# An instance norm on one core: the last pair of rows of each tile normalised by VectorE and ScalarE together

## The chip, the core and the metric

The kernel runs on one core of a Trainium2 chip. The time is device microseconds (us) for one execution of the whole kernel. Six runs of the kernel before took 5006.07, 5009.72, 4999.88, 4965.09, 4964.45 and 4966.33 us; the median is 4983.1 us. The profile is of one further execution, which took 4963.64 us.

Names used: DVE is VectorE, ACT is ScalarE, SP is SyncE (here it only issues transfers), DMA stands for the core's 16 DMA engines. HBM is the memory outside the core, SBUF the large memory inside it, PSUM the small one.

## The reference

```python
x: float32 [256, 256, 4096]          # np.random.randn
eps: 1e-5

mean = np.mean(x, axis=2, keepdims=True)
var = np.var(x, axis=2, keepdims=True)
return ((x - mean) / np.sqrt(var + eps)).astype(np.float32)
```

There are 65,536 independent rows of 4096 float32. Each row is read once from HBM and written once: 1073.74 MB in, 1073.74 MB out.

## The kernel before

**Tiles.** A tile holds 512 rows: 128 partitions with K = 4 rows each, 64 KB per partition, 8.39 MB in all. There are 128 tiles and three buffers (`X[0]` to `X[2]`) in SBUF. Tile t lives in buffer t mod 3, and the normalised rows overwrite the loaded ones.

**VectorE, per tile** (`vector_tile`). It waits for the load, then runs one pass per row (L86, four of them) that multiplies the row by 1/4096 in place and accumulates its sum, so that the row's mean comes out beside it. Then, for each pair of rows, it waits until ScalarE has the pair's standard deviation, takes the reciprocal (L97), works out minus mean times reciprocal (L99), and normalises the two rows in place with one multiply-add pass each (L108).

**ScalarE, per tile** (`scalar_tile`). As each row's mean arrives it squares the row's deviation from it and accumulates the sum (L132, output thrown away into `junk` in PSUM). After each second row it takes a square root over two columns (L141), which releases VectorE for that pair.

**SyncE** issues every transfer, all on one queue, in an order written out by hand. In the steady part it repeats: wait until tile t is done and store it (L155), then wait until the store of tile t-1 has landed, since that frees the buffer, and load tile t+2 into it (L160). The wait for "tile t is done" counts the four increments that the four L108 instructions give to `done`.

**Ends.** The first tile is loaded in two halves of two rows each, and the first and the last tile are computed and stored in halves (L171), so that the first store can begin early and the last store is short. At the start SyncE issues the two half loads, the load of tile 1, the two half stores of tile 0, the load of tile 2, and then goes on as above. At the end the last load is issued two tiles ahead, and the stores of the last three tiles follow.

Engines speak to one another only through semaphores: `loaded`, `means`, `stds`, `done`, `stored`. A semaphore called `scaled` is allocated and not used. `take` waits for a count and then clears the semaphore.

Of the kernel before, what the change touches and what calls it, by code (L numbers as in the profile page):

```python
# [10 lines left out]
def kernel(  # L11
# [9 lines left out]
    AF = mybir.ActivationFunctionType  # L21
    ALU = mybir.AluOpType
    P = 128
    K = 4
    BUFS = 3

    x_flat = x.flatten_outer_dims()
    out_flat = out.flatten_outer_dims()
    n, d = x_flat.shape
# [7 lines left out]
    half = K // 2  # L37
# [7 lines left out]
    junk = psum.tile([P, d], fp32)  # L45
    X = [pool.tile([P, K, d], fp32, name=f"x{s}") for s in range(BUFS)]
    mean, ss, std, rstd, nbias = (
        [pool.tile([P, K], fp32, name=f"{name}{s}") for s in range(BUFS)]
        for name in ("mean", "ss", "std", "rstd", "nbias")
    )  # L50
# [3 lines left out]

    loaded = [nc.alloc_semaphore(f"loaded{s}") for s in range(BUFS + 1)]
    stored = [nc.alloc_semaphore(f"stored{s}") for s in range(BUFS + 1)]
    own_v = nc.alloc_semaphore("own_v")
# [3 lines left out]
    scaled = nc.alloc_semaphore("scaled")  # L61
    done = [nc.alloc_semaphore(f"done{s}") for s in range(BUFS + 1)]
    ready = nc.alloc_semaphore("ready")

    def take(engine, sem, count):
        engine.wait_ge(sem, count)
        engine.sem_clear(sem)  # L67

    V, A, S = nc.vector, nc.scalar, nc.sync

    def vector_tile(s, r0=0, k=K, ld=None, dn=None):

        x = X[s]
        ld = loaded[s] if ld is None else ld
        dn = done[s] if dn is None else dn
        own = 0

        def mine(instruction):
            nonlocal own
            own += 1  # L80
            return instruction.then_inc(own_v, 1)

        if ld:
            take(V, ld, 16)
        for r in range(r0, r0 + k):
            V.tensor_scalar(  # L86
                out=x[:, r, :], in0=x[:, r, :], scalar1=1.0 / d, scalar2=None, op0=ALU.mult, op1=ALU.add,
                accum_out=mean[s][:, r : r + 1],
            ).then_inc(means, 1)
        for b in range(r0, r0 + k, 2):  # L90
            c = slice(b, b + 2)
            final = b == r0 + k - 2
            if final:
                take(V, stds, (b - r0) // 2 + 1)
            else:
                V.wait_ge(stds, (b - r0) // 2 + 1)
            mine(V.reciprocal(out=rstd[s][:, c], in_=std[s][:, c]))  # L97
            V.wait_ge(own_v, own)
            mine(V.scalar_tensor_tensor(  # L99
                out=nbias[s][:, c], in0=mean[s][:, c], scalar=-1.0 / d, in1=rstd[s][:, c], op0=ALU.mult, op1=ALU.mult  # L100
            ))
            if final:
                take(V, own_v, own)
            else:
                V.wait_ge(own_v, own)
            for r in range(b, b + 2):
                c = slice(r, r + 1)
                V.tensor_scalar(  # L108
                    out=x[:, r, :], in0=x[:, r, :], scalar1=rstd[s][:, c], scalar2=nbias[s][:, c],
                    op0=ALU.mult, op1=ALU.add,  # L110
                ).then_inc(dn, 1)

    def scalar_tile(s, r0=0, k=K, ld=None, dn=None):

        x = X[s]
        last = r0 + k - 1
        own = 0

        def mine(instruction):
            nonlocal own  # L120
            own += 1
            return instruction.then_inc(own_a, 1)

        for r in range(r0, last + 1):
            c = slice(r, r + 1)
            if own:
                A.wait_ge(own_a, own)
            if r == last:
                take(A, means, k)
            else:  # L130
                A.wait_ge(means, r - r0 + 1)
            mine(A.activation(  # L132
                out=junk, in_=x[:, r, :], func=AF.Square, bias=mean[s][:, c], scale=-float(d), accum_out=ss[s][:, c]
            ))
            if (r - r0) % 2:
                c = slice(r - 1, r + 1)
                if r == last:
                    take(A, own_a, own)
                else:
                    A.wait_ge(own_a, own)  # L140
                A.activation(  # L141
                    out=std[s][:, c], in_=ss[s][:, c], func=AF.Sqrt, bias=eps_tile, scale=1.0 / d**3
                ).then_inc(stds, 1)

    def rows_of(ap, t):

        if isinstance(t, int):
            return ap[t]
        first, period, count, i = t
        ap = ap[first : first + period * (count - 1) + 1 : period]  # L150
        return ap[bass.ds(i, 1)].rearrange("o p k d -> p (o k) d")

    def store(s, t):
        take(S, done[s], K)
        S.dma_start(out=rows_of(out_t, t), in_=X[s][:, :, :]).then_inc(stored[s], 16)  # L155

    def load(s, t, wait=True):
# [4 lines left out]
    def half_of(h):  # L162
        return slice(h * half, (h + 1) * half)

    def second(sems, s, h):
        return sems[BUFS] if h else sems[s]

    def store_half(s, t, h):
        r = half_of(h)
        take(S, second(done, s, h), half)  # L170
        S.dma_start(out=out_t[t][:, r, :], in_=X[s][:, r, :]).then_inc(second(stored, s, h), 16)  # L171

    def halves(tile_fn, s, first):
# [4 lines left out]
    last = ntiles - 1  # L178
# [3 lines left out]
    with tc.tile_critical():  # L182
        with nc.Block() as block:  # L183

            @block.sync
            def _(sync):
                for h in range(2):
                    r = half_of(h)
                    S.dma_start(out=X[0][:, r, :], in_=x_t[0][:, r, :]).then_inc(second(loaded, 0, h), 16)
                load(1, 1, wait=False)  # L190
                store_half(0, 0, 0)
                store_half(0, 0, 1)
                load(2, 2, wait=False)
                store(1, 1)
                take(S, stored[BUFS], 16)
                load(0, 3)

                with S.Fori(0, rounds) as i:
                    for t in range(L0, L0 + BUFS):
                        store(t % BUFS, (t, BUFS, rounds, i))  # L200
                        load((t + 2) % BUFS, (t + 2, BUFS, rounds, i))
                load(last % BUFS, last)
                store((last - 2) % BUFS, last - 2)
                store((last - 1) % BUFS, last - 1)
                store_half(last % BUFS, last, 0)
                store_half(last % BUFS, last, 1)
                for s in ((last - 2) % BUFS, (last - 1) % BUFS, last % BUFS, BUFS):
                    take(S, stored[s], 16)

            @block.vector  # L210
            def _(vector):
                V.memset(eps_tile, eps / d**2).then_inc(ready, 1)  # L212
                halves(vector_tile, 0, True)
                vector_tile(1)
                with V.Fori(0, rounds) as i:
                    for j in range(BUFS):
                        vector_tile((L0 + j) % BUFS)
                vector_tile((last - 2) % BUFS)
                vector_tile((last - 1) % BUFS)
                halves(vector_tile, last % BUFS, False)  # L220

            @block.scalar
            def _(scalar):
                take(A, ready, 1)
                halves(scalar_tile, 0, True)
                scalar_tile(1)
                with A.Fori(0, rounds) as i:
                    for j in range(BUFS):
                        scalar_tile((L0 + j) % BUFS)
                scalar_tile((last - 2) % BUFS)  # L230
                scalar_tile((last - 1) % BUFS)
                halves(scalar_tile, last % BUFS, False)
# [35 lines left out]
```

## Time and profile before

| what | value |
|---|---|
| median of six runs | 4983.1 us (4964.45 to 5009.72) |
| profiled execution, own time | 4963.64 us |
| its span, first to last instruction | 4961.6 us |
| DVE busy | 3506.0 us (71% of the span), 2049 instructions |
| ACT busy | 2024.4 us (41%), 1282 instructions |
| moved by DMA | 2147.52 MB, mean 433 GB/s |
| one L108 pass over 128x4096 (DVE) | 2410 ns |
| one L132 pass over 128x4096 (ACT) | 3678 ns |
| one L86 pass over 128x4096 (DVE) | 4416 ns |

A busy share is a share of the span in which the engine executed something. The digits of the slice rows are tenths: 9 stands for 90% or more of one fortieth of the span. "Issue to landing" of a transfer is the time from the moment SyncE issues it until its last byte is reported; it contains the time that the transfer spends behind others.

### The profile page before, as it was taken

How to read it: one execution, taken by the hardware profiler on the slowest of the kernel's cores; microseconds unless marked ns; L12 is line 12 of the kernel's file. 1: busy time of each engine (PE TensorE's matmuls, PEld its weight loads, DVE VectorE, ACT ScalarE, POOL GpSimd, SP SyncE). 2: the span in 40 equal slices, each digit the busy share in tenths (PEclk: the TensorE clock that was granted, in tenths of full speed). 3: DMA queues.
4: the chain of work that ended last, by engine and by line, in shares of the span. 5: the costliest groups of instructions: out<-in, count | busy, mean ns of one | idle time of the engine just before them, and what ended most of it. 6: DMA issues, size and time to landing. Idle time of an engine off the chain costs nothing.

```text
span 4961.6 us, 5694 instructions
## 1 busy us (share of the span) xinstructions
DVE 3506.0 (71%) x2049; ACT 2024.4 (41%) x1282; POOL 0.2 (0%) x4
## 2 busy tenths in 40 slices
DVE  6777767777677766777667776777767776677766
ACT  4444333443344433444334443344334443344433
POOL 0000000000000000000000000000000000000000
DMA  9999999999999999999999999999999999999999
GB/s 414 435 434 431 436 431 432 435 434 435 433 434 436 432 434 436 433 433 435 434 436 433 434 436 432 434 435 434 434 435 434 435 433 434 435 433 434 435 434 405
DMA packets 37298, 2147.52 MB, mean 433 GB/s; under 512 B 4144, under 2 KB 4144, under 8 KB 4144
## 3 DMA queue, kind: packets, MB, share of 16 engines
q1 hardware_dynamic: 37296, 2147.50, 100.0%
q14 instruction: 2, 0.02, 0.0%
HBM read 1073.74 MB, written 1073.74 MB: 433 GB/s over the span
## 4 chain that ended last, share of the span: by engine, by line
DMA 73%; DVE 25%; issue 1%; another core or an unknown queue 0%; ACT 0%; SPq 0%; DVEq 0%; ACTq 0%
DMA x<-in_x_dram 41%; DMA out_dram<-x 32%; DVE x L86 16%; DVE x L108 8%; DVE nbias L99 0%; ACT junk L132 0%; DVE rstd L97 0%; DVEq L67 0%; SPq L160 0%; SPq L155 0%; DVEq L183 0%; ACT std L141 0%; SPq L67 0%; ACT L141 0%
## 5 line engine op out<-in xcount | busy, mean ns | idle before, releaser
L86 DVE TENSOR_SCALAR_CACHE_REDUCE x<-x 128x4096 f32<-128x4096 f32 x512 | 2232.3, 4416 | 1383.9 <-DMA x<-in_x_dram 1383.9
L132 ACT ACTIVATE junk<-x,mean 128x4096 f32<-128x4096 f32 x512 | 1883.1, 3678 | 2897.2 <-DVE x L86 2897.2
L108 DVE TENSOR_SCALAR x<-x,rstd,nbias 128x4096 f32<-128x4096 f32 x512 | 1212.1, 2410 | 28.2 <-DVE nbias L99 10.9
L132 ACT ACTIVATION_READ_ACCUMULATOR junk<-x,mean 128x1 f32 x512 | 95.5, 186 | 0.0
L141 ACT ACTIVATE std<-ss,eps_tile 128x2 f32<-128x2 f32 x256 | 75.6, 295 | 19.1
L97 DVE RECIPROCAL rstd<-std 128x2 f32<-128x2 f32 x256 | 40.7, 159 | 19.4 <-ACT std L141 19.4
L99 DVE SCALAR_TENSOR_TENSOR nbias<-mean,rstd 128x2 f32<-128x2 f32 x256 | 41.2, 161 | 8.9
L86 DVE DVE_READ_ACCUMULATOR x<-x 128x1 f32 x512 | 42.3, 83 | 0.0
L132 ACT ACT_TABLE_LOAD x1 | 1.3, 1283 | 1.2 <-DVE eps_tile L212 1.2
L141 ACT ACT_TABLE_LOAD x1 | 1.3, 1283 | 0.1
L212 DVE MEMSET eps_tile<- 128x1 f32 x1 | 0.1, 59 | 1.0 <-SPq L182 1.0
L249 POOL MEMSET const-uint8-127<- 128x1 uint8 x1 | 0.1, 103 | 0.0
L249 POOL MEMSET const-bfloat16-1.0<- 128x1 bf16 x1 | 0.1, 101 | 0.0
L249 POOL MEMSET const-float32-0.0<- 128x1 f32 x1 | 0.1, 98 | 0.2 <-issue 0.2
L249 POOL MEMSET const-float32-1.0<- 128x1 f32 x1 | 0.1, 98 | 0.0
## 6 DMA issues: line engine op xcount, KB each, us to landing
out_dram<-x SPq DMA_DIRECT2D x4, 4096.0 KB, 16.4
x<-in_x_dram SPq DMA_DIRECT2D x2, 4096.0 KB, 16.6
x<-in_x_dram SPq DMA_DIRECT2D x127, 48.7
out_dram<-x SPq DMA_DIRECT2D x126, 30.0
```

The lines of the kernel that those rows point to most:

```text
L86: V.tensor_scalar(out=x[:, r, :], in0=x[:, r, :], scalar1=1.0 / d, scalar2=None, op0=ALU.mult, op1=ALU.add, accum_out=mean[s][:, r : r + 1 ...
L97: mine(V.reciprocal(out=rstd[s][:, c], in_=std[s][:, c]))
L99: mine(V.scalar_tensor_tensor(out=nbias[s][:, c], in0=mean[s][:, c], scalar=-1.0 / d, in1=rstd[s][:, c], op0=ALU.mult, op1=ALU.mult))
L108: V.tensor_scalar(out=x[:, r, :], in0=x[:, r, :], scalar1=rstd[s][:, c], scalar2=nbias[s][:, c], op0=ALU.mult, op1=ALU.add,).then_inc(dn, 1)
L132: mine(A.activation(out=junk, in_=x[:, r, :], func=AF.Square, bias=mean[s][:, c], scale=-float(d), accum_out=ss[s][:, c]))
L141: A.activation(out=std[s][:, c], in_=ss[s][:, c], func=AF.Sqrt, bias=eps_tile, scale=1.0 / d**3).then_inc(stds, 1)
L212: V.memset(eps_tile, eps / d**2).then_inc(ready, 1)
L249: nc = _bacc.Bacc("TRN2", target_bir_lowering=False, num_devices=1)
```

## The change

The last pair of rows that a call of `vector_tile` normalises (rows 2 and 3 of a whole tile, the only pair of a half tile) is shared. VectorE still normalises the pair's first row whole, but only the last 1024 columns of its second row. ScalarE takes the first 3072 columns of that row: after its last square root it waits for a new signal, `scaled`, which VectorE gives when the pair's scale and bias are ready, and runs one Identity activation with that scale and bias, in place. A tile therefore gives five increments to `done` instead of four (a half tile three instead of two), and the stores wait for five (three).

```diff
+    Q = 3072
 ...
                 take(V, own_v, own)
             else:
                 V.wait_ge(own_v, own)
+            if final:
+                V.sem_inc(scaled, 1)
             for r in range(b, b + 2):
                 c = slice(r, r + 1)
+                f = slice(Q, d) if r == r0 + k - 1 else slice(0, d)
                 V.tensor_scalar(
-                    out=x[:, r, :], in0=x[:, r, :], scalar1=rstd[s][:, c], scalar2=nbias[s][:, c],
+                    out=x[:, r, f], in0=x[:, r, f], scalar1=rstd[s][:, c], scalar2=nbias[s][:, c],
                     op0=ALU.mult, op1=ALU.add,
                 ).then_inc(dn, 1)
 ...
     def scalar_tile(s, r0=0, k=K, ld=None, dn=None):
 
         x = X[s]
+        dn = done[s] if dn is None else dn
 ...
                 A.activation(
                     out=std[s][:, c], in_=ss[s][:, c], func=AF.Sqrt, bias=eps_tile, scale=1.0 / d**3
                 ).then_inc(stds, 1)
+        c = slice(last, last + 1)
+        take(A, scaled, 1)
+        A.activation(
+            out=x[:, last, :Q], in_=x[:, last, :Q], func=AF.Identity, bias=nbias[s][:, c], scale=rstd[s][:, c]
+        ).then_inc(dn, 1)
 ...
     def store(s, t):
-        take(S, done[s], K)
+        take(S, done[s], K + 1)
 ...
-        take(S, second(done, s, h), half)
+        take(S, second(done, s, h), half + 1)
```

## The prediction, made before the result was known

> **What bounds the kernel now.** I read the page's slices first, then the queue and the chain, then one tile's time line, then the transfers at both ends.
>
> ```profile
> DMA  9999999999999999999999999999999999999999
> GB/s 414 435 434 431 436 431 432 435 434 435 433 434 436 432 434 436 433 433 435 434 436 433 434 436 432 434 435 434 434 435 434 435 433 434 435 433 434 435 434 405
> ...
> HBM read 1073.74 MB, written 1073.74 MB: 433 GB/s over the span
> ...
> DMA 73%; DVE 25%; issue 1%; another core or an unknown queue 0%; ACT 0%; SPq 0%; DVEq 0%; ACTq 0%
> ```
>
> The DMA engines are busy in every slice, and all slices but the two ends carry 431 to 436 GB/s. The chain, though, gives DVE a quarter of the span. These two must be reconciled: either the transfers are back to back and DVE only appears on the way to an early issue, or DVE's work is really in the loop that sets the period. One tile decides it:
>
> ```profile
> 2011.50 0.34 SPq L155 DMA_DIRECT2D out_dram<-x  x1
> 2012.08 0.35 SPq L160 DMA_DIRECT2D x<-in_x_dram  x1
> 2022.28 4.42 DVE L86 TENSOR_SCALAR_CACHE_REDUCE x<-x 128x4096 f32<-128x4096 f32 x1 [10.99 <-DMA x<-in_x_dram]
> ...
> 2045.18 4.73 DVE L108 TENSOR_SCALAR x<-x,rstd,nbias 128x4096 f32<-128x4096 f32 x2
> 2050.07 0.34 SPq L155 DMA_DIRECT2D out_dram<-x  x1
> 2050.64 0.35 SPq L160 DMA_DIRECT2D x<-in_x_dram  x1
> 2060.95 4.42 DVE L86 TENSOR_SCALAR_CACHE_REDUCE x<-x 128x4096 f32<-128x4096 f32 x1 [11.03 <-DMA x<-in_x_dram]
> ```
>
> and the issues, with KB or, where that is left out, count and median us to landing:
>
> ```profile
> x<-in_x_dram SPq DMA_DIRECT2D x127, 48.7
> out_dram<-x SPq DMA_DIRECT2D x126, 30.0
> ```
>
> The first store above is of tile t, the load behind it of tile t+2; the load of t+1, issued a period before, landed at 2022.28, when DVE's first pass on it starts. Adding the times to landing: store 2011.5 + 30.0 = 2041.5, load 2012.1 + 48.8 = 2060.9. So the landings are 2022.3, 2041.5, 2060.9: 19.2 to 19.4 us apart, whatever was issued when. One tile is 8.39 MB, and 8.39 MB in 19.3 us is 434 GB/s, the rate of the slices. The transfers run in issue order, one after the other, without a gap. When the store is issued at 2050.07, the load ahead of it still needs 10.9 us.
>
> How late may a store be before a gap opens? The nearest row is a transfer issued to a nearly empty queue, the second half store of tile 0:
>
> ```profile
> L171 SPq DMA_DIRECT2D out_dram<-x x1: 338/338/338, 51.5 to 51.5; - x1
> DMA to landing us min/median/max: 12.1/12.1/12.1
> ```
>
> 4.19 MB at 433 GB/s take 9.7 us, so issue to first byte costs about 12.1 - 9.7 = 2.4 us. The cover is 10.9 - 2.4 = 8.5 us per tile. The period is 38.64 us (2050.64 less 2012.08 is 38.56, and three tiles in the chain take 115.9), of which DVE works 28 and waits 11.0 for a load.
>
> **The change part by part.** Rows used:
>
> ```profile
> L132 ACT ACTIVATE junk<-x,mean 128x4096 f32<-128x4096 f32 x512 | 1883.1, 3678 | 2897.2 <-DVE x L86 2897.2
> L108 DVE TENSOR_SCALAR x<-x,rstd,nbias 128x4096 f32<-128x4096 f32 x512 | 1212.1, 2410 | 28.2 <-DVE nbias L99 10.9
> ...
> L141 ACT ACTIVATE std<-ss,eps_tile 128x2 f32<-128x2 f32 x256 | 75.6, 295 | 19.1
> ...
> L99 DVE SCALAR_TENSOR_TENSOR nbias<-mean,rstd 128x2 f32<-128x2 f32 x256 | 41.2, 161 | 8.9
> ```
>
> *DVE's part shrinks.* The slope between 128x2 at 161 ns and 128x4096 at 2410 ns is 0.549 ns an element, so 1024 columns cost about 0.16 + 0.56 = 0.72 us (0.60, a quarter of 2.41, to 2.41, no gain, are the ends). The pair, 4.73 us now, becomes 4.73 - 2.41 + 0.72 = 3.04: 1.69 us less. The added signal is one queue step, 0.03 us by the chain's DVEq pieces.
>
> *ACT's part appears.* No row shows an Identity from SBUF to SBUF. Between 128x2 at 295 ns and 128x4096 at 3678 ns the slope is 0.826 ns, so 3072 columns cost 0.295 + 2.54 = 2.83 us; the ends are three quarters of 3.68, 2.76, and a whole 3.68. It starts about 0.1 us after VectorE's signal and ends at 2.9, beside DVE's 3.04. So `done` completes about 1.7 us earlier in each tile, 1.0 at ACT's dear end, 0 at DVE's. The new wait on ACT stands after the last square root; queued behind it is the next tile's first L132, before which ACT sits idle for 21 us anyway, so it delays nobody. On SP the wait for `done` holds up the store and, behind it, the load of t+2; both go out when the later of the two engines is ready.
>
> *Table loads.* Square runs after the square root without reloading (one ACT_TABLE_LOAD of 1283 ns for each of L132 and L141 in the whole run). The changed kernel as built has the same two. Were Identity to need its own, two more per tile, 2.57 us, would fit in the 8.5 of cover.
>
> The Trainium skill, "ScalarE: Activation LUTs", section "Rules for kernel authors", says to put multiplies and adds on VectorE and not on ScalarE, which speaks against this edit. The rows agree on the price: 0.55 ns an element on DVE against 0.83 on ACT. By the rule alone ACT's 3072 columns are a loss of 0.85 us of engine time a tile; run beside each other they are a gain of 1.7. On the end of the run both sums give nothing while the cover holds.
>
> *What it is worth in the steady part: 0.* The store joins the queue 1.7 us earlier, waits there 1.7 us longer, and lands when it would have. The load behind it likewise.
>
> *Head.* The first half store was issued at 33.06 and landed 20.0 later, at 53.06. Back to back the second would land 9.7 later, at 62.8; it landed at 51.5 + 12.1 = 63.6. So the queue stood empty for 0.8 us. DVE's stretch there is its own: half 0 ends 1.69 earlier, half 1 twice that, 3.4, so the issue moves to 48.1, is ready at 50.5, and the gap closes. All later landings shift by it: **-0.8 us**.
>
> *Tail.* The store of tile 126 is issued at 4910.61 and lands 30.3 later, at 4940.9; the half stores of tile 127 land at 4929.04 + 21.6 = 4950.6 and 4947.5 + 12.8 = 4960.3. The spacing is 9.7 and 9.7: back to back to the end. DVE's last work could come 5.1 us earlier (three shortened pairs) and nothing would land earlier: **0**.
>
> *Can ACT's writes slow the transfers?* Not shown before: ACT writes PSUM there. The nearest row is DVE writing the same buffers: averaged over 54 tiles the rate is 428 GB/s in the 10 us in which DVE and ACT are idle and 420 in the 10 us of the L108 passes. At that -1.8%, 2.83 us x 130 calls cost 6.6 us; since the stretches between show 429 and 466, I put this down to packets counted in whole, take 0, and keep 6.6 for the range. On the other side, the first slice's shortfall against 434 GB/s is 124 us x 20/434 = 5.7 us, of which start-up (0.96 to the first issue, 2.4 to the first byte) is 3.3; no more than 2.4 can be gaps that the change closes.
>
> **Sum.** 4963.64 - 0.8 = 4962.8 for the profiled execution, with ends at -2.4 and +6.6. That execution lies at the low end of the six runs; their median is 4983.1, so on its scale the forecast is **4982.3 us**, a change of -0.02%.
>
> The Trainium skill, "DMA: Bandwidth & Descriptors", section "Specifications", gives a fabric ceiling of 435 GB/s and an HBM limit of about 358 GB/s for a core. The measured 433 refutes the second for this run (by it the transfers alone would take about 6000 us, an estimate) and stands at the first; by 435 GB/s the transfers need an estimated 4937 us and no edit of compute could win more than half a per cent.
>
> **Rivals.**
> 1. *The chain is right and DVE is in the loop.* If a load always took 48.8 us from its issue, two loads would be in flight and the period would be (48.8 + 28.4) / 2 = 38.6, which fits as well. Then 1.7 us less per tile gives 0.85 per period, 128 x 0.85 = 108 us: 4874. For it: the chain's 25% and that fit. Against: landings evenly 19.3 apart, a 4.19 MB store landing in 12.1 us with little ahead of it and 21.6 behind others, and no slice with room. Chance 0.03.
> 2. *Slower: ACT's in-place pass over SBUF takes rate from the transfers.* Place: the 2.83 us of Identity in each tile. It decides (1%, 50 us) from 0.39 us a tile, a loss of 12% of the rate during the pass; at a quarter it costs 2.83 x 0.25 / 0.75 = 0.94 us, 130 times, 123 us: 5105. For it: no spare rate to hide anything, and the operation isn't in the profile. Against: L86 and L108 write the same SBUF for 27 of 38.6 us at full rate. Chance 0.04.
> 3. *The gain doesn't exist:* ACT wakes late or its pass takes 3.7 us or more, so the pair ends no earlier. Then the head's 0.8 stays too: 4983. Part of the forecast's case.
>
> **How the numbers follow.** Forecast (with rival 3) 0.93, rival 1 0.03, rival 2 0.04. These are also the chances of same, faster and slower; 1% is about what a measurement of this kernel can tell from no change. Both rivals are left out of the range, which is set by the spread of the runs, far wider than the terms: 4964.45 - 2.4 rounded down to 4960 below, 5009.72 rounded to 5010 above.
>
> **What would show it.** DVE busy falls by 130 x 1.69 = 220 to about 3286 us, ACT rises by 130 x 2.83 = 368 to about 2392. DVE's wait for loads grows from 1383.9 to about 1600. The medians to landing *grow*, stores from 30.0 to about 31.7, loads from 48.7 to about 50.4, while the middle slices stay at 431 to 436 GB/s. Times to landing that stay at 30.0 and 48.7 with a period near 37.8 would mean rival 1; slices below 430 where ACT runs Identity, rival 2. The prediction is wrong if the transfers were not at their limit, or if ACT's writes reach them.

## The result, and the profile after

| | runs | median us | range us |
|---|---|---|---|
| kernel before | 65 | 5007.81 | 4963.55 to 5018.0 |
| changed kernel | 30 | 4962.82 | 4961.15 to 5010.17 |

The ratio is 0.9944, 95% interval 0.9925 to 0.9962: the changed kernel is faster by about half a per cent. The median alone says more than that, because the runs of the kernel before fall mostly into two groups, one near 4965 us and one near 5010 us. In this comparison 45 of 65 runs of the kernel before were at or above 4995 us, and 4 of 30 of the changed kernel. The lower groups, the runs below 4995, differ by 2 us (medians 4964.75 and 4962.67). The two profiled executions are both of the lower group: 4963.64 us before, 4962.77 after.

The page of the changed kernel, slices, groups and transfers (the group rows give busy us and mean ns of one, then the idle time before; the last two rows end with the median us from issue to landing):

```profile
GB/s 423 430 434 434 431 437 433 431 436 434 432 437 434 434 434 434 434 435 433 434 435 433 435 434 433 436 434 432 437 434 434 434 434 434 435 433 435 435 432 404
...
L87 DVE TENSOR_SCALAR_CACHE_REDUCE x<-x 128x4096 f32<-128x4096 f32 x512 | 2232.3, 4416 | 1580.4 <-DMA x<-in_x_dram 1580.4
...
L112 DVE TENSOR_SCALAR x<-x,rstd,nbias 128x4096 f32<-128x4096 f32 (+1 forms) x512 | 1004.2, 2004 | 33.9 <-DVE nbias L100 29.3
L151 ACT ACTIVATE x<-x,nbias,rstd 128x3072 f32<-128x3072 f32 x130 | 383.2, 2948 | 146.2 <-DVEq L68 146.2
...
x<-in_x_dram SPq DMA_DIRECT2D x127, 50.3
out_dram<-x SPq DMA_DIRECT2D x126, 31.5
```

The middle slices carry what they carried. What VectorE won it spends waiting for loads (1580.4 us, 1383.9 before), and each transfer is issued 1.5 us earlier and waits 1.5 to 1.6 us longer. One tile in the time line shows the shared pair:

```profile
2043.08 3.13 DVE L112 TENSOR_SCALAR x<-x,rstd,nbias 128x4096 f32<-128x4096 f32 x2 [0.18 <-DVE nbias L100]
2043.10 2.95 ACT L151 ACTIVATE x<-x,nbias,rstd 128x3072 f32<-128x3072 f32 x1 [1.14 <-DVEq L68]
2046.36 0.34 SPq L165 DMA_DIRECT2D out_dram<-x  x1
2046.94 0.35 SPq L170 DMA_DIRECT2D x<-in_x_dram  x1
2058.78 4.42 DVE L87 TENSOR_SCALAR_CACHE_REDUCE x<-x 128x4096 f32<-128x4096 f32 x1 [12.57 <-DMA x<-in_x_dram]
```

Both engines start within 0.02 us of each other and end within 0.2 us. The store is issued 12.4 us before the load ahead of it lands; before the change it was 10.9.

So one execution of the lower group behaves as forecast. What had to be found out is why the kernel before so often isn't in the lower group, and the changed one nearly always is.

### The profile page after: what moved, and what is told of

Same layout as the page of the kernel before. It is cut to its first block, busy times and chain, and to the rows that moved or that the text cites. A ratio compares the mean times of both kernels' runs of the same rounds, so it can differ in the third digit from the quotient of the medians.

```text
span 4960.5 us, 5954 instructions
## 1 busy us (share of the span) xinstructions
DVE 3298.0 (66%) x2049; ACT 2407.7 (49%) x1412; POOL 0.2 (0%) x4
## 4 chain that ended last, share of the span: by engine, by line
DVE 62%; another core or an unknown queue 31%; issue 4%; DMA 2%; ACT 0%; DVEq 0%; ACTq 0%; SPq 0%
DVE x L87 44%; DVE x L112 17%; DMA x<-in_x_dram 1%; DVE nbias L100 1%; DMA out_dram<-x 1%; DVE rstd L98 1%; ACT junk L137 0%; DVEq L68 0%; DVEq L225 0%; ACT L146 0%; ACT std L146 0%; DVEq L193 0%; ACTq L68 0%; ACTq L67 0%
## 5 line engine op out<-in xcount | busy, mean ns | idle before, releaser
L87 DVE TENSOR_SCALAR_CACHE_REDUCE x<-x 128x4096 f32<-128x4096 f32 x512 | 2232.3, 4416 | 1580.4 <-DMA x<-in_x_dram 1580.4
L137 ACT ACTIVATE junk<-x,mean 128x4096 f32<-128x4096 f32 x512 | 1883.1, 3678 | 2367.2 <-DVE x L87 2367.2
L112 DVE TENSOR_SCALAR x<-x,rstd,nbias 128x4096 f32<-128x4096 f32 (+1 forms) x512 | 1004.2, 2004 | 33.9 <-DVE nbias L100 29.3
L151 ACT ACTIVATE x<-x,nbias,rstd 128x3072 f32<-128x3072 f32 x130 | 383.2, 2948 | 146.2 <-DVEq L68 146.2
L137 ACT ACTIVATION_READ_ACCUMULATOR junk<-x,mean 128x1 f32 x512 | 95.5, 187 | 0.0
L146 ACT ACTIVATE std<-ss,eps_tile 128x2 f32<-128x2 f32 x256 | 75.6, 295 | 19.1
## 6 DMA issues: line engine op xcount, KB each, us to landing
x<-in_x_dram SPq DMA_DIRECT2D x127, 50.3
out_dram<-x SPq DMA_DIRECT2D x126, 31.5
```

The costliest lines, as they stand in the source:

```text
L87: V.tensor_scalar(out=x[:, r, :], in0=x[:, r, :], scalar1=1.0 / d, scalar2=None, op0=ALU.mult, op1=ALU.add, accum_out=mean[s][:, r : r + 1 ...
L112: V.tensor_scalar(out=x[:, r, f], in0=x[:, r, f], scalar1=rstd[s][:, c], scalar2=nbias[s][:, c], op0=ALU.mult, op1=ALU.add,).then_inc(dn, 1)
L137: mine(A.activation(out=junk, in_=x[:, r, :], func=AF.Square, bias=mean[s][:, c], scale=-float(d), accum_out=ss[s][:, c]))
L146: A.activation(out=std[s][:, c], in_=ss[s][:, c], func=AF.Sqrt, bias=eps_tile, scale=1.0 / d**3).then_inc(stds, 1)
L151: A.activation(out=x[:, last, :Q], in_=x[:, last, :Q], func=AF.Identity, bias=nbias[s][:, c], scale=rstd[s][:, c]).then_inc(dn, 1)
```

## The experiments

Theory 1, that of the prediction: transfers are back to back in both kernels, and what separates 4965 from 5010 us lies outside the kernel. Theory 2: it is the time at which the store reaches the queue. A transfer is carried by 16 DMA engines, a sixteenth each, and it counts as landed when the last is through. The trace keeps the 16 completions of each transfer apart; in mid-run of the profiled execution of the kernel before, the first came 6.5 us ahead of the last (5.8 in that of the changed kernel). This lead belongs to an execution as much as to a kernel: two later executions of the changed kernel had 7.2 and 6.0, one of the kernel before 6.2. Seen from the first engine, the queue runs dry 6.5 us earlier than the landing tells.

### The change again, given back, and by another way

> The changed kernel as it is, beside the kernel before on the same chip. Theory 1 (the transfers are back to back in both, and what separates runs near 4963 us from runs near 5010 us lies outside the kernel): both kernels fall into the same group in the same round, ratio 0.999 to 1.001. Theory 2 (a store issued 1.5 to 1.7 us earlier keeps more work queued, and that keeps the transfers at their best rate): the changed kernel is near 4963 us in most runs and the kernel before near 5010 us in most, ratio near 0.991 to 0.995.

Given back: a reduction on VectorE, in the changed kernel, ahead of the pair.

```diff
+    spare = pool.tile([P, 1], fp32)
 ...
+            if final:
+                mine(V.tensor_reduce(out=spare, in_=x[:, b, :1600], op=ALU.add, axis=AX.X))
             if final:
                 take(V, own_v, own)
```

> The changed kernel, with an added reduction of about 1.7 us on VectorE ahead of the shared pair, so that the store goes out when it did before, while ScalarE still does its pass in place. The reduction's sum is thrown away. Theory 1: as the kernel before, ratio 1.000 within 0.001. Theory 2: the gain goes with the time given back, the kernel falls into the same group as the kernel before, ratio 0.999 to 1.001, where the changed kernel has 0.991 to 0.995. If ScalarE's pass itself made the difference, it would stay near 4963 us.

The early store without ScalarE: the kernel before with a shorter last pass.

```diff
+    Q = 3072
 ...
+                f = slice(Q, d) if r == r0 + k - 1 else slice(0, d)
                 V.tensor_scalar(
-                    out=x[:, r, :], in0=x[:, r, :], ...
+                    out=x[:, r, f], in0=x[:, r, f], ...
```

> The kernel before, with the last row's pass of each pair cut to its last 1024 columns and nothing on ScalarE: the other 3072 columns of that row leave the kernel without being normalised. The store goes out about 1.7 us earlier. Theory 1: ratio 1.000 within 0.001. Theory 2: as the changed kernel, near 4963 us, ratio 0.991 to 0.995.

The other direction: the kernel before with a longer reduction.

```diff
+    spare = pool.tile([P, 1], fp32)
 ...
+            if final:
+                mine(V.tensor_reduce(out=spare, in_=x[:, b, :3600], op=ALU.add, axis=AX.X))
```

> The kernel before, with an added reduction of about 3.8 us on VectorE ahead of the last pair of each call (its sum is thrown away), so that the store goes out 3.8 us later and the time for which the queue has work falls from 8.5 to about 4.7 us. Theory 1: no gap opens, ratio 1.000 within 0.002. Theory 2: all runs near 5010 us or slower, since the first of the 16 shares of a transfer lands 6.5 us before the last one and would find its queue empty.

All four ran beside 29 runs of the kernel before (10 at or above 4995 us, the others with a median of 4965.2):

| kernel | runs | at or above 4995 | median of the others, us | ratio, 95% interval |
|---|---|---|---|---|
| e1_after | 12 | 0 | 4963.0 | 0.9956 (0.9926 to 0.9985) |
| e2_given_back | 12 | 1 | 4965.8 | 0.9976 (0.9943 to 1.0009) |
| e3_cover_only | 12 | 0 | 4963.2 | 0.9958 (0.9928 to 0.9988) |
| e4_less_cover | 6 | 6 | none; all 5031.75 to 5040.44 | 1.0103 (1.0056 to 1.015) |

e3_cover_only has no work on ScalarE beyond the squares and behaves as the changed kernel, to 0.2 us. So the earlier store alone is enough, whoever does the pass. Whether the gain goes when the time is given back stays undecided: e2_given_back loses the 2 us of the lower group again (4965.8), but has 1 run of 12 in the upper group and not 4, and its ratio decides nothing. e4_less_cover refutes what theory 1 says of it, that no gap opens. The prediction gave a store 8.5 us of cover before a gap opens; 3.9 us of it were taken, and every run lost 67 to 75 us against the lower group. About 20 of them are lost at the two ends of the run, the rest between them (see the table of stretches below). The page of e4_less_cover:

```profile
GB/s 383 428 434 434 433 426 432 425 432 426 432 425 427 432 432 427 427 431 428 430 429 430 425 433 425 426 433 425 433 425 433 425 431 428 425 433 425 433 427 377
...
L104 DVE TENSOR_REDUCE spare<-x 128x1 f32<-128x3600 f32 x130 | 506.5, 3896 | 0.0
...
x<-in_x_dram SPq DMA_DIRECT2D x127, 45.8
out_dram<-x SPq DMA_DIRECT2D x126, 26.6
```

and one tile of its time line:

```profile
2043.10 0.34 SPq L158 DMA_DIRECT2D out_dram<-x  x1
2043.68 0.35 SPq L163 DMA_DIRECT2D x<-in_x_dram  x1
2050.14 4.42 DVE L87 TENSOR_SCALAR_CACHE_REDUCE x<-x 128x4096 f32<-128x4096 f32 x1 [7.25 <-DMA x<-in_x_dram]
```

The store still goes out 7.0 us before the load ahead of it lands, more than the 2.4 us from issue to first byte. By landings the queue never runs dry in mid-run, and yet the middle slices fall to 425 to 434 GB/s. DMA is still "busy" in all slices.

### Half stores, and small delays

In e5_half_stores the kernel before stores every whole tile in two transfers (left out here: the wait for such a store to land counts 32 increments instead of 16):

```diff
-        take(S, done[s], K)
-        S.dma_start(out=rows_of(out_t, t), in_=X[s][:, :, :]).then_inc(stored[s], 16)
+        S.wait_ge(done[s], half)
+        S.dma_start(out=rows_of(out_t, t)[:, :half, :], in_=X[s][:, :half, :]).then_inc(stored[s], 16)
+        take(S, done[s], K)
+        S.dma_start(out=rows_of(out_t, t)[:, half:, :], in_=X[s][:, half:, :]).then_inc(stored[s], 16)
```

> The kernel before, but every whole tile is stored in two halves, the first as soon as the first pair of rows is done, about 5.1 us earlier than the whole store now; the second half and the next load go out when they do now. Theory 2 (what counts is that the queue holds work when the first of the 16 shares of a transfer is through, 5 to 7 us ahead of the last): nearly all runs near 4962 us, ratio as e3_cover_only, 0.992 to 0.997, depending on how many runs of the kernel before are near 5010. Theory 4 (what counts is when the whole store and the load behind it are issued, the loop through VectorE): as the kernel before, ratio 1.000 within 0.003.

e6_delay_1us has the added reduction of e4_less_cover over 1000 columns instead of 3600.

> The kernel before with an added reduction of about 1.1 us on VectorE ahead of the last pair of each call (its sum is thrown away). Theory 2: the store finds the queue with 7.4 us of cover instead of 8.5, the group near 4963 us is not reached any more: most runs 5005 to 5025 us, between the kernel before and the 5037 us of e4_less_cover. Theory 1 (nothing in the kernel): as the kernel before.

e7_both has the same half stores in the changed kernel.

> The changed kernel with the half stores of e5_half_stores. Theory 2: cover to spare from both, all runs within 3 us of 4962, no better than e5_half_stores, since the transfers alone take about 4952 us. Theory 4: as the changed kernel.

e8_half_stores_late has both the half stores and the 3600 columns, on the kernel before.

> The half stores of e5_half_stores with the 3.9 us reduction of e4_less_cover ahead of the last pair: the second half store and the next load go out as late as in e4_less_cover, but the first half store goes out early. Theory 2: near 4963 us. Theory 4: near 5037 us, as e4_less_cover.

Beside 35 runs of the kernel before (10 at or above 4995 us, median of the others 4965.4):

| kernel | runs | at or above 4995 | median of the others, us | ratio, 95% interval |
|---|---|---|---|---|
| e5_half_stores | 12 | 1 | 4972.5 | 0.9988 (0.9958 to 1.0018) |
| e6_delay_1us | 12 | 2 | 4968.6 | 0.9984 (0.9952 to 1.0016) |
| e7_both | 12 | 4 | 4970.6 | 1.0002 (0.9968 to 1.0036) |
| e8_half_stores_late | 12 | 1 | 4990.5 | 1.0025 (0.9998 to 1.0052) |

Not all of this went as theory 2 said. e6_delay_1us moved its lower group up by 3 us but did not lose it. Half stores cost about 7 us on their own account (126 more transfers), and with work queued early e7_both still had 4 of 12 runs at 5005 to 5011 us, which is against theory 2. e8_half_stores_late was 46 us better than e4_less_cover and 18 us worse than e5_half_stores:

```profile
2018.33 0.33 SPq L158 DMA_DIRECT2D out_dram<-x  x1
2027.35 0.33 SPq L160 DMA_DIRECT2D out_dram<-x  x1
2027.93 0.58 SPq L165 DMA_DIRECT2D x<-in_x_dram  x1
2034.35 4.42 DVE L87 TENSOR_SCALAR_CACHE_REDUCE x<-x 128x4096 f32<-128x4096 f32 x1 [7.22 <-DMA x<-in_x_dram]
```

Here the first half store goes out 16.0 us before the load lands, the second half and the next load 7.0 and 6.4 us before it, as late as the store and the load of e4_less_cover. The slices of e5_half_stores, e6_delay_1us and e8_half_stores_late show where time was lost:

```profile
GB/s 414 431 431 433 434 429 433 436 432 433 431 434 437 432 432 433 434 436 434 431 432 433 434 434 432 433 434 434 433 430 434 434 434 433 431 432 434 433 434 409
GB/s 405 437 431 435 433 431 434 434 435 434 434 433 435 435 434 435 433 433 434 434 433 432 433 435 433 433 434 433 436 433 434 435 432 434 435 434 436 432 436 402
GB/s 387 431 432 433 431 434 431 434 436 431 433 432 434 433 434 430 433 435 434 433 432 434 433 434 430 433 434 435 431 432 433 436 430 432 433 436 432 433 431 379
```

Beside e5_half_stores, e8_half_stores_late loses in the first and the last slice and not between them. The landings of the loads of tile 10 and tile 127 cut each profiled execution into three stretches (us; the landings are those of the traces' semaphore records):

| execution | start to landing of tile 10 | tile 10 to tile 127 | from there to the end |
|---|---|---|---|
| before | 396.5 | 4505.5 | 59.6 |
| changed | 395.1 | 4505.8 | 59.6 |
| e6_delay_1us | 399.8 | 4506.3 | 61.2 |
| e5_half_stores | 397.7 | 4513.9 | 59.8 |
| e8_half_stores_late | 404.9 | 4515.0 | 69.7 |
| e11_delay_2us (below) | 402.7 | 4554.2 | 64.5 |
| e4_less_cover | 407.3 | 4557.8 | 68.7 |

So the 18 us by which e8_half_stores_late lies above e5_half_stores are 7.2 at the start, 9.9 at the end and 1.1 between: in this execution, as in 11 of its 12 runs, an early first half repairs the whole loss of the middle, and the expectation's theory 4, by which the whole store and the load behind it set the time, falls. The 3 us of e6_delay_1us are of the ends as well (4.9 us in this execution; 0.8 between). Beyond the price of half stores (8.4 us), only e11_delay_2us and e4_less_cover lose in the middle, 48.7 and 52.3 us. Each row is one execution, and every one but those of e11_delay_2us and e4_less_cover belongs to its kernel's lower group.

### A control, and two more doses

e9_before_again and e10_after_again are the two kernels unchanged.

> The kernel before, unchanged, run as if it were a variant. If a run near 5010 us is a property of the kernel's own timing (theory 2), about a third of these runs lie there, as in the runs of the kernel before of the last two comparisons (23 of 64 at or above 4995). If it is a property of the place that the kernel before has in a comparison, or of the moment (theory 1), these runs lie there as seldom as those of the variants so far, about 1 in 10.

> The changed kernel once more, beside e9_before_again. Theory 2: at most 1 or 2 of 12 near 5010 us, the others 4962 to 4964, 2 us below the lower group of the kernel before. Theory 1: as many near 5010 us as e9_before_again.

e11_delay_2us has the added reduction over 2200 columns.

> The kernel before with an added reduction of about 2.4 us on VectorE ahead of the last pair (its sum is thrown away). If the lateness of the store acts through a threshold near the 5 to 7 us by which the first share of a transfer is ahead of the last, the lower group rises steeply between e6_delay_1us (1.2 us, 4968) and e4_less_cover (3.9 us, 5037): here 4980 to 5015. If only whole gaps count (the 8.5 us of cover of the prediction), 4965.

e12_more_cover is e3_cover_only with both rows of the last pair cut:

```diff
-                f = slice(Q, d) if r == r0 + k - 1 else slice(0, d)
+                f = slice(Q, d) if final else slice(0, d)
```

> The kernel before with both rows of the last pair cut to their last 1024 columns: the first 3072 columns of those two rows are not normalised. The store goes out about 3.4 us earlier. Theory 2: no run near 5010 us, all at 4961 to 4963, no better than the changed kernel since the transfers are at their limit. Theory 1: about as e9_before_again.

The control decides little: e9_before_again had 1 of 6 runs in the upper group beside 3 of 11 of the kernel before. (The 23 of 64 in its expectation include three runs between 4988 and 4992; at or above 4995 there were 20.) e10_after_again had none of 6, all at 4961.87 to 4963.16. In the two comparisons that hold both kernels, the kernel before was at or above 4995 in 13 of 40 runs and the changed one in 0 of 18. All doses together, ordered by how much earlier the store of a tile is issued (the kernel before in all three sets of experiments, 10 of 29, 10 of 35 and 3 of 11 runs):

| kernel | store issued earlier by, us | runs | at or above 4995 | median of the others, us |
|---|---|---|---|---|
| e12_more_cover | 3.2 | 6 | 0 | 4962.9 |
| e3_cover_only | 1.6 | 12 | 0 | 4963.2 |
| changed kernel (e1, e10) | 1.5 | 18 | 0 | 4962.8 |
| before, beside them | 0 | 75 | 23 | 4965.3 |
| e6_delay_1us | -1.2 | 12 | 2 | 4968.6 |
| e11_delay_2us | -2.4 | 6 | 4 (5022 to 5024) | 4976.3 |
| e4_less_cover | -3.9 | 6 | 6 (5032 to 5040) | none |

The first three shifts are the growth of the store's median time to landing, the last three the duration of the added reduction. e11_delay_2us has both groups again, far apart: 4976 and 5022. Its profiled execution is of the upper one, 5023.36 us. The ends of that execution are 6.2 and 4.9 us longer than those of the kernel before, and 11.1 us is what its lower group lies above 4965; that the lower group loses nothing in the middle is thus likely, but none of its runs was profiled. The page of the profiled execution:

```profile
GB/s 401 428 433 434 432 433 432 429 431 428 432 427 428 431 427 427 430 431 431 428 430 429 429 428 433 426 427 431 428 427 433 427 430 430 427 427 431 429 427 390
...
L104 DVE TENSOR_REDUCE spare<-x 128x1 f32<-128x2200 f32 x130 | 316.7, 2436 | 0.0
...
x<-in_x_dram SPq DMA_DIRECT2D x127, 47.3
out_dram<-x SPq DMA_DIRECT2D x126, 27.9
```

It begins at 433 GB/s and drops to 427 to 433 after a tenth of the run, and stays there. e12_more_cover, whose store goes out 3.2 us earlier than before, shows the full rate to the end and a correspondingly longer wait:

```profile
GB/s 422 431 433 434 431 433 434 432 437 432 433 438 431 434 437 431 433 438 431 434 437 433 434 435 433 436 433 432 438 432 433 438 432 433 437 431 434 437 432 406
...
x<-in_x_dram SPq DMA_DIRECT2D x127, 51.9
out_dram<-x SPq DMA_DIRECT2D x126, 33.2
```

Twice the lead of the changed kernel is worth nothing more: 4962.9.

Where the time goes in the middle can be worked out from the trace's record of packets. Nearly all 64 KB packets of the kernel before take 2418 ns. The table has, between the landings of tile 10 and tile 127, what the 64 KB packets took above that, per DMA engine; the share of 1000 to 4000 us in which fewer than 16 packets were under way, so that an engine had none; and the lead of the first share of a load over the last:

```
                         longer packets   fewer than 16   first share ahead of last, loads
before                    1.8 us          0.0%            6.5 us
changed                   1.4             0.0             5.8
e6_delay_1us              4.2             0.0             5.6
e11_delay_2us            49.1             0.4             7.1
e4_less_cover            51.9             0.5             5.7
```

So the 48.7 and 52.3 us of the middle are nearly all longer packets. Engines without a packet, which theory 2 expects, are met in the two executions that lost time in the middle and not in the other three, but they stand for a few us of it at most. 47% of the 1391 packets of e11_delay_2us over 2.5 us (300 to 4850 us) begin 30 to 38 us after a load's landing. Its store is issued about 30.4 us after that landing and could start 2.4 us later, at 32.8, while the first engine is through with the load ahead of it about 38.9 - 7.1 = 31.8 us after it. The late store and the first idle engine meet there. The other half begin 8 to 14 us after a landing, where nothing of the sort is known; e6_delay_1us, which lost nothing in the middle, has 264 such packets, and 96% of them at 30 to 38 us.

## Why the prediction was right, and where it was not

The forecast was no change, 4982.3 us with 4960 to 5010; measured were 4962.82 and a ratio of 0.9944. For an execution of the lower group the sum was right: 4962.8 forecast, 4962.77 measured. The effect on the median was missed, and that the median lies in the range all the same is luck: the range was drawn to hold both groups of runs, not because one of them might become rare. Step by step:

- *DVE's and ACT's parts.* VectorE's pair takes 3.13 us (3.04 forecast, 4.73 before), ScalarE's pass 2.948 (2.83). Busy 3298.0 and 2407.7 us (3286 and 2392 forecast). The Trainium skill, "ScalarE: Activation LUTs", section "What ACT_TABLE_LOAD costs", adds 93 ns for each per-partition operand of an activation; the Identity has two where the square has one, and the row is indeed 0.12 us above the estimate. That page's rule against multiplies and adds on ScalarE was no guide: the pass is dearer there, and the tile is done 1.5 us sooner because both run at once.
- *Table loads.* None was added: the page has one each for L137 and L146, and none for L151. That step holds.
- *The store joins the queue earlier and waits longer.* Stores 31.5 us to landing (31.7 forecast), loads 50.3 (50.4), VectorE's wait for loads 1580 us (about 1600), slices unchanged. In the profiled execution this step holds, and rival 1 falls: times to landing did not stay, and 108 us were not won.
- *Head, -0.8, and tail, 0.* In the changed kernel the load of tile 3 was issued at 74.9 and landed 46.7 later, at 121.6; before, at 79.5 + 43.7 = 123.2. So the head was worth 1.6 us, where 0.8 was forecast. From the landing of tile 127 on, both executions take 59.6 us, as the tail of 0 has it. Of the whole, 0.9 was left between the two profiled executions, 4963.64 and 4962.77.
- *Can ACT's writes slow the transfers?* No: the rate is the same, and e1_after and e3_cover_only, with and without these writes, are 0.2 us apart. Rival 2 falls.
- *"The cover is 10.9 - 2.4 = 8.5 us per tile."* **This is the step that failed.** It counts to the last of 16 completions. The first comes 6.5 us earlier in that execution, so for the engine that is ahead the cover of the kernel before is about 8.5 - 6.5 = 2.0 us. The doses bracket it, though not sharply: e6_delay_1us takes 1.2 us, was in the upper group no more often than the kernel before beside it (2 of 12, 10 of 35), and in its profiled execution loses 0.8 us in the middle. e11_delay_2us takes 2.4 and was in the upper group in 4 of 6 runs, e4_less_cover takes 3.9 and was there in 6 of 6; their profiled executions lose 48.7 and 52.3 us in the middle, where a cover of 8.5 would have left 6.1 and 4.6 us to spare. The Trainium skill, "DMA: Bandwidth & Descriptors", section "Queues, rings and completion order", says that a copy is split over as many as 16 rings, one for each DMA engine, each worked through by itself; the traces agree, with the first and the last share of one transfer 4.1 to 7.2 us apart in mid-run of the 14 profiled executions. The prediction did not use this for the cover.
- *"Which is set by the spread of the runs."* The prediction took the distance between 4964 and 5010 us as something that the change would leave alone, and put the profiled execution's 0.8 us on the scale of the median. In the later comparisons with both kernels the upper group was met in 13 of 40 runs before and 0 of 18 after, and the lower groups are only 2 us apart, so most of the gain is in how often a run leaves the lower group.

What stays open: no profiled execution of the kernel before fell into its upper group, so that its 45 us are the same stretched packets as in e11_delay_2us is argued from the doses and not shown. By its shares the kernel before has 2 us of cover left, so why it falls into the upper group at all is open too. How often it does changed from one comparison to the next (45 of 65, 10 of 29, 10 of 35, 3 of 11), and 4 of the first 30 runs of the changed kernel did too, so something besides the kernel takes part. The three sets of experiments ran on three different chips, and the lead of the first share differs between executions of one kernel; neither was tested as a cause. And e7_both, with more work queued than any other, had 4 such runs of 12, so a queue that holds work is not the whole condition: that the early store makes the upper group rare is shown, how it does so is not. What makes packets take longer was not found.

## What to carry to other kernels

Where transfers are the limit, count the cover of an issue to the moment when the first of a transfer's shares is through, not to its landing: here 2 us were left where the landings showed 8.5. An edit that shortens work behind full queues can then pay without moving the rate of a good run, by keeping runs good; look at the spread of the runs, not only at a profiled one. Past that point more lead was worth nothing (e12_more_cover), and a second transfer per tile to gain it cost more than it brought here. And before a few us are put down to the steady part, cut the run into its ends and its middle: a delay in each tile also lengthens the first and the last stretch.

## What the runs showed of the hardware that was not expected

- The 16 shares of one 8.39 MB transfer drift apart and stay apart: 0.4 us in the first transfers, 5.8 and 6.5 us in mid-run of the two kernels' profiled executions, while landings stay 19.32 us apart. Another execution of the changed kernel had 7.2 us, at the same speed.
- The page shows DMA "busy" in every slice at 427 GB/s as at 434: a packet that takes longer counts as busy. The rate is the row to read, and 1 to 1.5% of it is the whole effect.
- One and the same kernel can settle at either of two speeds within one set of runs: e11_delay_2us at 4976 and 5022 us, nothing between in six runs.
